# The mixer's output projection of an encoder layer by seven block products, with the operands' forms in the buffers of the normed input

## The chip, the cores and the metric

The kernel runs on one core of one Trainium2 chip. The metric is the time of one execution in microseconds of the device, from the start of the program to its end. A change of about 0.2% can be told from none. All inputs and weights lie in HBM as float32; the weights are packed on the host into blocks of 128 partitions x 1024 columns.

## The reference, cut to what matters

One encoder layer on 512 tokens of width 1024, with 256 memory tokens:

```python
# per layer
x = x + token_mixer(rmsnorm(x, norm_mix), ...)       # 4 HGRN2 heads and 4 mLSTM heads, each 128 wide
x = x + cross_attention(rmsnorm(x, norm_xattn), rmsnorm(mem, norm_mem), w_q, w_kv, w_o)
x = x + squared_relu_mlp(rmsnorm(x, norm_mlp), w_up, w_down)
return rmsnorm(x, norm_final)

# the last line of token_mixer: the projection that the change is about
return jnp.concatenate([hgrn_out, mlstm_out], axis=-1) @ w_out     # (512 x 1024) @ (1024 x 1024)
```

`cross_attention` takes its keys and values from the memory tokens by `w_kv`, its queries from `rmsnorm(x)` by `w_q`, and projects its heads by `w_o`. The mixer's heads are scans over chunks in the reference; the kernel computes them in blocks of 128 tokens.

## The kernel before

**Precision.** Every large matmul is done as three: both operands are split into a high part (a rounding copy on ScalarE) and a low part (the difference, on VectorE), and high x high, high x low and low x high are added in one PSUM bank. `split_out` (line 258) is the split, `mm3` (lines 260 to 263) the three matmuls. Rows of both engines at L258 are therefore splits, of weights (`wh`, `wl`) or of activations.

**Weights.** `SEQ` is the order in which weight blocks come. `load(i)` has SP fetch block i into one of three `st` buffers (L236); `split(i)` makes its `wh` and `wl`, three buffers each; `weights` asks for a block and two more ahead.

**Chains.** The heads are generators (`hgrn_pair`, `mlstm_chain`) in the list `chains`; the projections call `tick()` every few matmuls, which moves one of two chains on by a step. So the heads' small operations stand among the matmuls of a projection, and a scheduler then sets the order on each engine. `drain()` runs what is left.

**Stages around the change.** 0 to 240 us: input projection and HGRN heads. 240 to 318 us: the mLSTM heads' queries and keys (`qk_proj`, with a convolution in `conv_evac`, L746), then the memory's keys (`kv`, eight products of 128x256 whose PSUM banks `mm` are split into the buffers `a4`) and values (four of 128x512), with the first two mLSTM heads beside them. An mLSTM head is: decay rows (L774, L777, L779, buffer `as`), four value products (L789, buffers `sm`), a denominator by tiny operations on VectorE and the GpSimd power (L795 to L802, L197, L199), and `head_out`: scale (L595), four transposes (L602), gate (L603), and the split of the result into `ys[idx]`, a `yT` buffer. `ys[0..3]` are the HGRN heads, `ys[4..7]` the mLSTM heads, each with 128 features on the partitions and 512 tokens in columns, high and low part beside each other.

318 to 349 us: the memory's values and the third and fourth mLSTM head. From 349 us: the output projection, `proj_res("out", ...)` at line 949. It goes over two halves of the output's columns, and in each over four row tiles of 128 tokens, with 8 k tiles of 128 features: the first half takes k tiles 0 to 3 (the HGRN heads) for all row tiles first, then `heads_done` drains the chains, then k tiles 4 to 7. Each finished 128x512 bank is added to the residual `xr[t, c]` (L924, buffers `vv`), its squares are summed on ScalarE, and four transposes turn it into `x2T` (L938, buffers `xT`), which the query projection `xq` of the cross-attention reads.

**Buffers.** PSUM has four `mm` and four `sm` banks. In SBUF there are two `xT` pairs-of-halves (first the normed input `xs`, last read by `qk_proj(1)`, then `x2T`), ten `a4` of 128x1024, two `gate` of 128x1024 (the gates of two HGRN or mLSTM heads each; the last two mLSTM heads read theirs until their L603), two `as`.

**By blocks.** The cross-attention's output projection (`xo`) and the second matrix of the MLP (`down`) are already done by `by_blocks`: a product of 2x2 blocks (tokens in two halves, features in two halves, columns in two halves) from seven products of blocks instead of eight. Some of the seven have a block as an operand, others a sum of blocks; sums of weight blocks are made by POOL DMAs that add into a buffer (`add_block`, L1065), sums of the heads by VectorE where the heads are made. Each product adds its result into one or two of the four output blocks (`INTO`).

Of the kernel before, what the change touches and what calls it, by code (L numbers as in the profile page):

```python
# [18 lines left out]
P = 128  # L19
# [26 lines left out]
def _split_order():  # L46
# [15 lines left out]
    seq += t("out", 0, 0) + t("out", 0, 512)  # L62
# [8 lines left out]
    seq += t("xo", 0, 512, 2)  # L71
# [5 lines left out]
NSTREAM = len(SEQ) - 10  # L77
# [3 lines left out]
def trunk(ctx: ExitStack, tc: tile.TileContext, x, mem, wpk, vec, cst, lmask, rmask, rows, out):  # L81
# [505 lines left out]
    def head_out(o, gate, gcol, idx):  # L587
# [17 lines left out]
        split_out(ys[idx][0], ys[idx][1], gate)  # L605
        yield

# [146 lines left out]
    def mlstm_chain(h, gate):  # L754
# [28 lines left out]
        for wt in range(4):  # L783
# [19 lines left out]
            if wt % 2 == 1:  # L803
                yield
        yield from head_out(ho, gate, V_MN + h, 4 + h)


    hst = {}
    pace = [2]
    scored = set()  # L810
# [76 lines left out]
    list(qk_proj(1))  # L887
    mlstm_start(1, mo1)
# [13 lines left out]

    xr = {}
# [6 lines left out]
    def heads_done():  # L910
        drain()
        load_xr(1)

    load_xr(0)
# [4 lines left out]

    def proj_res(mat, k0, src, tgt, st, pre=None, late=False):  # L920

        for c in range(2):
            for t, ps in proj_t(mat, k0, 512 * c, src, pre=pre if c == 0 else None, late=late and c == 0):
                v.tensor_tensor(out=xr[t, c], in0=ps, in1=xr[t, c], op=ALU.add)  # L924
                stats(st, t, c)
                transp(tgt, t, c)

    def transp(tgt, t, c):
        dst, gcol = tgt
        ps = smb()  # L930
        for k in range(4):
            pe.transpose(ps[:, k * P:k * P + P], xr[t, c][:, k * P:k * P + P], ident)
        for k in range(4):
            g = vc[:, gcol + 4 * c + k:gcol + 4 * c + k + 1]
            hi = dst[c][:, k * 1024 + t * P:k * 1024 + t * P + P]
            lo = dst[c][:, k * 1024 + 512 + t * P:k * 1024 + 512 + t * P + P]
            sc.activation(hi, ps[:, k * P:k * P + P], AF.Copy, scale=g)
            v.scalar_tensor_tensor(out=lo, in0=ps[:, k * P:k * P + P], scalar=g, in1=hi.bitcast(F32), op0=ALU.mult, op1=ALU.subtract)  # L938
# [9 lines left out]
    x2T = XT()  # L948
    proj_res("out", 0, ys, (x2T, V_XATTN), st1, heads_done, True)
# [86 lines left out]

    ORDER = ("P1", "P2", "P6", "P5", "P7", "P3", "P4")
    LATE = [(p, g) for p in ORDER[2:] for g in range(2)]  # L1040
    JOBS = {f: [("P1", 0), ("P2", 0), ("P1", 1), ("P2", 1)] + LATE for f in range(4)}

    JOBS[-1] = [(p, g) for p in ("P1", "P7", "P2", "P5", "P6", "P3", "P4") for g in range(2)]
    jobs_hl, sums, q_made = {}, {}, [None]

    def block(f, g, kh, c):
        return SIDX["t", "down" if f >= 0 else "xo", max(f, 0) * 8 + 2 * g + 4 * kh, 512 * c]

    def sum_loads(f, names):

        parts = {"T2": ((0, 1), (1, 1), (0, 0)), "U": ((0, 1), (0, 0)), "T3": ((0, 1), (1, 1))}
        for nme in names:
            if nme == "T3":
                t2 = [G4()[:, :] for _ in range(2)]
            else:
                t = A16()
                t2 = [t[:, g * 1024:g * 1024 + 1024] for g in range(2)]
            for g in range(2):
                sums[f, nme, g] = t2[g]
        return [add_block(sums[f, nme, g], block(f, g, *parts[nme][i]), i > 0)  # L1060
                for i in range(3) for nme in names for g in range(2) if i < len(parts[nme])]

    def add_block(dst, idx, accumulate=True):
        kw = dict(accum_op=ALU.add) if accumulate else {}
        return gp.dma_start(out=dst, in_=wpk[idx], **kw)  # L1065
# [5 lines left out]
    def job(f, n):  # L1071

        if n >= len(JOBS[f]):
            if f < 3:
                split(SIDX["d", "up", 0, 1024 * (f + 1)] + n - len(JOBS[f]))
# [350 lines left out]
```

## Time and profile before

| what | value |
|---|---|
| time, median of 3 runs | 847.56 us (847.48 to 848.4) |
| the profiled execution's own time | 847.43 us |
| its span in the trace | 845.3 us |
| granted TensorE clock, mean | 0.998 |
| HBM read, written | 116.00 MB, 2.10 MB |
| VectorE weight splits (L258, 128x1024 from `st`) | 131, mean 1224 ns |
| ScalarE's part of them | 131, mean 1060 ns |

How to read it: the span runs from the first to the last instruction; the 2 us between it and the execution's time lie around it. A busy share is the share of the span in which an engine had an instruction running. TensorE's matmuls are pipelined, so that a matmul shows a longer busy time than the step to the next one. In a timeline each row has the start, the busy time, engine, source line, operation, output and inputs, and in brackets the idle time ahead of the instruction with what ended it. In a table of windows each row has the length, and then for PE, PEld (weight loads), DVE (VectorE), ACT (ScalarE) and POOL the busy time with its number of instructions, the granted clock, the DMA share and GB/s.

### The profile page before, as it was taken

The page shows a single profiled execution, that of the slowest core. Times are in us where ns is not written, and L with a number is a line of the kernel's source. Part 1 is how long each engine was busy: PE and PEld are TensorE (multiplying, and loading weights), DVE is VectorE, ACT ScalarE, POOL GpSimd, SP SyncE. Part 2 cuts the span into 40 slices and gives each one's busy share as a digit, 9 for nine tenths or more (in the row PEclk, how much of TensorE's full clock was granted, in tenths as well). Part 3 has the DMA queues.
Part 4 walks back from the last instruction along what each step waited for, and adds up shares of the span by engine and source line. Part 5 has one row for each costly group of instructions (what it writes and reads, how often), then busy time and mean ns, then how long its engine had stood idle before and what let it go on. Part 6 is the DMA issues. An engine that isn't in the chain of part 4 may idle for free.

```text
span 845.3 us, 11740 instructions
## 1 busy us (share of the span) xinstructions
PE 834.2 (99%) x4434; PEld 689.3 (82%) x4434; DVE 589.3 (70%) x1025; ACT 433.6 (51%) x779; POOL 77.5 (9%) x130
## 2 busy tenths in 40 slices
PE   8999999999999999999999999999999999999996
PEld 6787888887977987888888888888888888888885
DVE  6568875599457987655557896776677656866685
ACT  5246454443578576454455575543454444434544
POOL 2000000100010000100010004103101210221001
PEclk9999999999999999999999999999999999999999
DMA  7342124122152332452261447968935993698332
GB/s 275 111 131 86 65 77 133 43 88 86 64 149 75 101 125 100 152 147 77 89 160 50 100 100 263 261 173 238 279 107 136 278 257 100 166 278 210 114 79 100
DMA packets 34122, 118.86 MB, mean 141 GB/s; under 512 B 3921, under 2 KB 4049, under 8 KB 34066
## 3 DMA queue, kind: packets, MB, share of 16 engines
q1 hardware_dynamic: 22832, 77.80, 26.8%
q0 software_dynamic: 10944, 39.85, 21.2%
q8 instruction: 35, 0.57, 0.3%
q10 hardware_dynamic: 290, 0.47, 0.2%
q14 instruction: 21, 0.17, 0.1%
HBM read 116.00 MB, written 2.10 MB: 140 GB/s over the span
## 4 chain that ended last, share of the span: by engine, by line
PE 90%; issue 5%; DVE 2%; DMA 1%; ACT 1%; POOL 1%; POOLq 0%; ACTq 0%; DVEq 0%
PE mm L261 18%; PE mm L262 18%; PE mm L263 18%; PE sm L1118 6%; PE sm L1116 6%; PE sm L1117 6%; PE sm L485 2%; PE sm L789 2%; PE mm L1118 2%; PE mm L1116 2%; PE mm L1117 2%; PE sm L774 2%; PE sm L555 2%; PE sm L263 1%; PE sm L262 1%
## 5 line engine op out<-in xcount | busy, mean ns | idle before, releaser
L258 ACT ACTIVATE wh<-st 128x1024 fp32r<-128x1024 f32 x131 | 138.6, 1060 | 190.2 <-PE mm L262 119.0
L258 DVE TENSOR_TENSOR wl<-st,wh 128x1024 fp32r<-128x1024 f32 x131 | 160.1, 1224 | 86.7 <-ACT wh L258 85.8
L261 PE MATMUL mm<-xT,wh 128*128 128x512 f32 x544 | 216.1, 398 | 0.0
L262 PE MATMUL mm<-xT,wh 128*128 128x512 f32 x544 | 212.8, 391 | 0.3 <-DVE xT L938 0.3
L263 PE MATMUL mm<-xT,wl 128*128 128x512 f32 x544 | 212.7, 391 | 0.1
L262 PEld LDWEIGHTS mm<-xT,wh 128*128 128x128 f32 x544 | 102.2, 188 | 22.1 <-issue 1.0
L263 PEld LDWEIGHTS mm<-xT,wl 128*128 128x128 f32 x544 | 102.1, 188 | 21.9 <-DVE wl L258 0.3
L261 PEld LDWEIGHTS mm<-xT,wh 128*128 128x128 f32 x544 | 102.2, 188 | 21.8 <-issue 0.7
L1065 POOL DMA_DIRECT2D as<-in_wpk x52 | 39.7, 765 | 250.8 <-DVE wl L258 165.8
L1305 DVE SCALAR_TENSOR_TENSOR t<-mm,rg 128x512 f32<-128x512 f32 x32 | 22.0, 691 | 52.2 <-PE mm L263 52.0
L1116 PE MATMUL sm<-wh,yT 128*128 128x512 f32 x128 | 49.8, 389 | 0.0
L1117 PE MATMUL sm<-wl,yT 128*128 128x512 f32 x128 | 49.8, 389 | 0.0
L1118 PE MATMUL sm<-wh,yT 128*128 128x512 f32 x128 | 49.8, 389 | 0.0
L258 ACT ACTIVATE wh<-as 128x1024 fp32r<-128x1024 f32 x26 | 27.6, 1062 | 37.0 <-PE sm L1118 23.7
L258 DVE TENSOR_TENSOR wl<-as,wh 128x1024 fp32r<-128x1024 f32 x26 | 31.9, 1226 | 14.0 <-ACT wh L258 14.0
L199 POOL TENSOR_TENSOR tiny<-tiny,misc 128x4 f32<-128x4 f32 (+1 forms) x10 | 9.6, 964 | 269.0 <-DVE tiny L197 269.0
L1116 PE MATMUL sm<-wh,a 128*128 128x512 f32 x84 | 32.9, 391 | 0.0
L1118 PE MATMUL sm<-wh,a 128*128 128x512 f32 x84 | 32.7, 389 | 0.0
L1117 PE MATMUL sm<-wl,a 128*128 128x512 f32 x84 | 32.7, 389 | 0.0
L1248 DVE TENSOR_TENSOR vv<-vv,sm 128x512 f32<-128x512 f32 x48 | 31.0, 680 | 1.7 <-PE sm L1118 1.7
L1117 PEld LDWEIGHTS sm<-wl,yT 128*128 128x128 f32 x128 | 24.0, 188 | 5.0
L1118 PEld LDWEIGHTS sm<-wh,yT 128*128 128x128 f32 x128 | 24.0, 188 | 5.0
(316 smaller groups left out, 1590.3 us busy)
## 6 DMA issues: line engine op xcount, KB each, us to landing
st<-in_wpk SPq DMA_DIRECT2D x131, 512.0 KB, 3.4
as<-in_wpk POOLq DMA_DIRECT2D x52, 512.0 KB, 7.0
gate<-in_wpk POOLq DMA_DIRECT2D x24, 512.0 KB, 7.2
as<-in_x SPq DMA_DIRECT2D x4, 512.0 KB, 6.7
vv<-in_x SPq DMA_DIRECT2D x8, 256.0 KB, 3.4
out<-vv SPq DMA_DIRECT2D x7, 256.0 KB, 2.2
a<-in_mem SPq DMA_DIRECT2D x2, 512.0 KB, 4.2
t<-in_rows SPq DMA_DIRECT2D x2, 256.0 KB, 4.9
```

The costliest lines, as they stand in the source:

```text
L258: return sc.activation(dst_hi, src, AF.Copy), v.tensor_tensor(out=dst_lo, in0=src, in1=dst_hi.bitcast(F32), op=ALU.subtract)
L261: pe.matmul(ps, lhsT=ah, rhs=bh, start=first, stop=False)
L262: pe.matmul(ps, lhsT=ah, rhs=bl, start=False, stop=False)
L263: pe.matmul(ps, lhsT=al, rhs=bh, start=False, stop=last)
L485: mm = pe.matmul(ps[64 * i:64 * i + 64, z:z + 64], lhsT=kc[j][:, w * P + 64 * i:w * P + 64 * i + 64], rhs=rhs(j, w * P, i), start=True, st ...
L555: pe.matmul(ps[:, t * P:t * P + P], lhsT=A[j][:, s * 512 + t * P:s * 512 + t * P + P], rhs=vh[s][:, h * P:h * P + P], start=(s == 0), stop ...
L1065: return gp.dma_start(out=dst, in_=wpk[idx], **kw)
L1116: pe.matmul(ps, lhsT=ah, rhs=bh, start=new, stop=False, **fl)
L1117: pe.matmul(ps, lhsT=ah, rhs=bl, start=False, stop=False, **fl)
L1118: pe.matmul(ps, lhsT=al, rhs=bh, start=False, stop=end and k == 1, **fl)
L1248: added = v.tensor_tensor(out=z, in0=z, in1=ps, op=ALU.add if sign > 0 else ALU.subtract)
L1305: v.scalar_tensor_tensor(out=y, in0=ps, scalar=0.0, in1=rrow[:, 0:512], op0=ALU.max, op1=ALU.mult)
```

## The change

The output projection of the mixer is done by `by_blocks`, as `xo` and `down` are, under the number -2: seven products in the order P1, P7, P2, P5, P6, P3, P4, each as two jobs of 12 matmuls (`g`: two k tiles each), on heads p and 4 + p as the two halves of the features. Its parts:

- `mix_start` makes from each HGRN head the difference of its token halves (first the sum of high and low part, L619, then the difference, L620, then a split into the buffer `xT`). It is called after `qk_proj(1)`, when the normed input is no longer read, and the two `xT` buffers taken then become `x2T` later.
- `mix_forms`, at the end of `head_out` of each mLSTM head, makes the three other forms (five operations of 256 columns, L633 to L637, and two splits), also into `xT`.
- The weight sums are T3 and U, in two halves (g) each. Of T3 the first half, and of U the first half in part, are added by POOL DMAs. The second half of each is made by `quick_sum`: two loads by SP and an addition on VectorE (L1175). That of U is loaded into a `gate` buffer.
- Each product adds its bank into the residual (L1113), 18 additions in all where there were 8; the transposes are made for two row tiles at a time; the first two column blocks of `xq` are taken together with the halves of the features in reversed order (`first_two`, which was the MLP's own).
- The order of the `out` weight blocks in `SEQ` is another, and two of them are no longer in the stream.

```diff
+        if idx >= 4:
+            formers.append((idx - 4, gate))
+            mix_forms()
...
+    def mix_start():
+        for p in range(4):
+            h, l = [t.bitcast(F32) for t in ys[p]]
+            e = T2()[:, 0:512]
+            v.tensor_tensor(out=e, in0=h, in1=l, op=ALU.add)
+            v.tensor_tensor(out=e[:, 0:256], in0=e[:, 0:256], in1=e[:, 256:512], op=ALU.subtract)
+            s3 = mixT[0][:, p * 512:p * 512 + 256], mixT[0][:, p * 512 + 256:p * 512 + 512]
+            split_out(*s3, e[:, 0:256])
+            sta_m[p].update(P1=tuple(t[:, 0:256] for t in ys[p]), P7=s3)
...
+    def mix_forms():
+        while mixT and formers:
+            p, m = formers.pop(0)
...
+            v.tensor_tensor(out=sa1, in0=x2h, in1=m2, op=ALU.subtract)
+            v.tensor_tensor(out=sa1, in0=sa1, in1=x2l, op=ALU.add)
+            v.scalar_tensor_tensor(out=sa2, in0=eh, scalar=-1.0, in1=m2, op0=ALU.mult, op1=ALU.subtract)
+            v.tensor_tensor(out=sa2, in0=sa2, in1=el, op=ALU.subtract)
+            v.tensor_tensor(out=s4, in0=m1, in1=sa2, op=ALU.add)
+            ya = mixT[1][:, p * 1024:p * 1024 + 1024]
+            split_out(ya[:, 0:512], ya[:, 512:1024], sa)
...
+            split_out(yh, yl, s4)
...
     list(qk_proj(1))
+    x2T = XT()
+    mixT += x2T
+    mix_start()
+    mix_forms()
     mlstm_start(1, mo1)
...
+    JOBS[-2] = JOBS[-1] = [(p, g) for p in ("P1", "P7", "P2", "P5", "P6", "P3", "P4") for g in range(2)]
...
+    sums[-2, "T3", 0] = G4()[:, :]
+    add_block(sums[-2, "T3", 0], block(-2, 0, 0, 1), False)
+    add_block(sums[-2, "T3", 0], block(-2, 0, 1, 1))
...
-    proj_res("out", 0, ys, (x2T, V_XATTN), st1, heads_done, True)
...
+    def quick_sum(nme, g, t, b0, b1):
+        other = A16()[:, 0:1024]
+        for dst, b in ((t, b0), (other, b1)):
+            nc.sync.dma_start(out=dst, in_=wpk[block(-2, g, *b)])
+        v.tensor_tensor(out=t, in0=t, in1=other, op=ALU.add)
+        sums[-2, nme, g] = t[:, :]
+
+    def mix_ready(p, g):
+        if (p, g) == ("P1", 0):
+            while len(valued) < 4:
+                tick1()
+            quick_sum("T3", 1, A4(), (0, 1), (1, 1))
+            sums[-2, "U", 0] = A4()[:, :]
+            nc.sync.dma_start(out=sums[-2, "U", 0], in_=wpk[block(-2, 0, 0, 1)])
+        if (p, g) == ("P7", 1):
+            load_xr(1)
+        if (p, g) == ("P2", 0):
+            drain()
+            add_block(sums[-2, "U", 0], block(-2, 0, 0, 0))
+            quick_sum("U", 1, G4(), (0, 1), (0, 0))
+            while waiting:
+                waiting.pop(0)()
+            fixed.enter_context(tc.manual_schedule(engines={mybir.EngineType.PE}))
...
+    by_blocks(-2, sta_m, (mm2, mm2, sm2, sm2), add_1, mix_ready, mix_after)
```

How the change moves instructions is seen on three engines. First VectorE while the memory's keys are projected. `as_331` is a decay buffer of the first mLSTM head (its line L779 before is L820 after), `a4` the buffers of the keys, `mm` their PSUM banks, `t2` the scratch of the forms, `xT_365` the buffer that the forms go to. Before:

```order
L779 TENSOR_TENSOR as_331_2273<-as_331_2273,sm_364_2474 128x512
L795 TENSOR_SCALAR tiny_375_2508<-sm_374_2502 128x2
L751 SCALAR_TENSOR_TENSOR yT_342_2344<-t2_362_2462,t2_361_2458 128x512
L796 TENSOR_TENSOR tiny_375_2508<-tiny_375_2508,sm_374_2502 128x2
L258 TENSOR_TENSOR a4_365_2478<-mm_372_2488,a4_365_2478 128x256
L258 TENSOR_TENSOR wl_416_2718<-st_405_2666,wh_415_2717 128x1024
```

After, from the same operation to the same bank's split (here `mm_378`):

```order
L820 TENSOR_TENSOR as_331_2273<-as_331_2273,sm_364_2474 128x512
L619 TENSOR_TENSOR t2_367_2480<-yT_204_1413 128x512
L792 SCALAR_TENSOR_TENSOR yT_342_2344<-t2_362_2462,t2_361_2458 128x512
L258 TENSOR_TENSOR wl_422_2740<-st_411_2688,wh_421_2739 128x1024
L620 TENSOR_TENSOR t2_367_2480<-t2_367_2480 128x256
L619 TENSOR_TENSOR t2_368_2485<-yT_214_1486 128x512
L258 TENSOR_TENSOR xT_365_2478<-t2_367_2480,xT_365_2478 128x256
L620 TENSOR_TENSOR t2_368_2485<-t2_368_2485 128x256
L619 TENSOR_TENSOR t2_369_2490<-yT_288_2085 128x512
L258 TENSOR_TENSOR xT_365_2478<-t2_368_2485,xT_365_2478 128x256
L620 TENSOR_TENSOR t2_369_2490<-t2_369_2490 128x256
L619 TENSOR_TENSOR t2_370_2495<-yT_290_2107 128x512
```

All sums (L619) and three differences (L620) of the HGRN heads' forms stand here, with two of their splits into `xT_365`. On the same engine it goes on without a gap:

```order
L258 TENSOR_TENSOR wl_434_2813<-st_423_2743,wh_433_2812 128x1024
L258 TENSOR_TENSOR xT_365_2478<-t2_369_2490,xT_365_2478 128x256
L620 TENSOR_TENSOR t2_370_2495<-t2_370_2495 128x256
L836 TENSOR_SCALAR tiny_381_2530<-sm_380_2524 128x2
L258 TENSOR_TENSOR a4_371_2500<-mm_378_2510,a4_371_2500 128x256
```

Where three rows stood between the decay's product and the split of the bank, there are now fifteen: the forms of the four HGRN heads with three of their splits, the convolution's product, two weight splits and a tiny operation.

TensorE in the same stage: `mm_424` is the fourth product of the keys, `mm_436` the fifth, which takes the bank that the split above empties; `sm_391` before and `sm_397` after are the first value products of the first mLSTM head. Before, where the fourth product (there `mm_418`) ends:

```order
L261 MATMUL mm_418_2723<-a4_312_2173,wh_387_2573 128x256
L789 MATMUL sm_391_2592<-vv_249_1813,as_325_2233 128x129
L789 MATMUL sm_391_2592<-vv_250_1822,as_325_2233 128x129
L789 MATMUL sm_391_2592<-vv_252_1857,as_325_2233 128x129 x2
L789 MATMUL sm_391_2592<-vv_253_1866,as_325_2233 128x129
L262 MATMUL mm_418_2723<-a4_312_2173,wh_387_2573 128x256
```

After (six more matmuls of `mm_436`, on `a4_309`, stand directly ahead of the first row, and the last of `mm_424` ahead of them):

```order
L261 MATMUL mm_436_2818<-a4_310_2171,wh_409_2684 128x256
L262 MATMUL mm_436_2818<-a4_310_2171,wh_409_2684 128x256
L263 MATMUL mm_436_2818<-a4_310_2171,wl_410_2685 128x256
L261 MATMUL mm_436_2818<-a4_310_2171,wh_409_2684 128x256
L830 MATMUL sm_397_2614<-vv_249_1813,as_325_2233 128x129
L830 MATMUL sm_397_2614<-vv_250_1822,as_325_2233 128x129
L830 MATMUL sm_397_2614<-vv_252_1857,as_325_2233 128x129 x2
L830 MATMUL sm_397_2614<-vv_253_1866,as_325_2233 128x129
```

The value products now stand behind the first ten matmuls of the fifth key product, where they stood inside the fourth.

The third place is VectorE in the output projection, where U's second half is made: `gate_569` is the buffer that the weights are loaded to, `gate_282` the same memory as the gates of the last two mLSTM heads, `vv` the residual, `mm` and `sm` the products' banks. Before, in the second half of the columns:

```order
L924 TENSOR_TENSOR vv_524_3288<-mm_530_3297,vv_524_3288 128x512
L938 SCALAR_TENSOR_TENSOR xT_527_3294<-sm_554_3413,vc_68,xT_527_3294 128x128 x2
L938 SCALAR_TENSOR_TENSOR xT_527_3294<-sm_556_3441,vc_68,xT_527_3294 128x128 x2
L924 TENSOR_TENSOR vv_525_3290<-mm_531_3298,vv_525_3290 128x512
L938 SCALAR_TENSOR_TENSOR xT_527_3294<-sm_556_3441,vc_68,xT_527_3294 128x128 x2
```

After, from the last form on:

```order
L637 TENSOR_TENSOR t2_556_3417<-gate_282_2059,t2_555_3416 128x256
L258 TENSOR_TENSOR xT_366_2479<-t2_555_3416,xT_366_2479 128x512
L258 TENSOR_TENSOR xT_365_2478<-t2_556_3417,xT_365_2478 128x256
L1113 TENSOR_TENSOR vv_564_3452<-vv_564_3452,sm_557_3428 128x512
L1113 TENSOR_TENSOR vv_535_3334<-vv_535_3334,sm_557_3428 128x512
L1113 TENSOR_TENSOR vv_565_3454<-vv_565_3454,sm_558_3429 128x512
L1113 TENSOR_TENSOR vv_536_3336<-vv_536_3336,sm_558_3429 128x512
L1175 TENSOR_TENSOR gate_569_3479<-gate_569_3479,as_570_3480 128x1024
L1113 TENSOR_TENSOR vv_533_3330<-vv_533_3330,mm_571_3488 128x512
L1113 TENSOR_TENSOR vv_534_3332<-vv_534_3332,mm_572_3489 128x512
L258 TENSOR_TENSOR wl_576_3507<-gate_569_3479,wh_575_3506 128x1024
```

The last reader of the old gates, the sum into the same memory and the split of the sum stand in this order, with additions into the residual between them.

More of the change, by code (lines that the diff above doesn't have):

```diff
@@ L900, in trunk, with block @@
             mvx[t, c] = d
+    ORDER = ("P1", "P2", "P6", "P5", "P7", "P3", "P4")
+    LATE = [(p, g) for p in ORDER[2:] for g in range(2)]
+    JOBS = {f: [("P1", 0), ("P2", 0), ("P1", 1), ("P2", 1)] + LATE for f in range(4)}
+    JOBS[-2] = JOBS[-1] = [(p, g) for p in ("P1", "P7", "P2", "P5", "P6", "P3", "P4") for g in range(2)]
+    jobs_hl, sums, q_made, waiting = {}, {}, [None], []
+    def block(f, g, kh, c):
+        return SIDX["t", "down" if f >= 0 else "xo" if f == -1 else "out", max(f, 0) * 8 + 2 * g + 4 * kh, 512 * c]
@@ L1049, in sum_loads @@
[L1049 to L1061, printed above, removed]
```

354 lines of the change are left out of this document (188 added, 166 removed).

## The prediction

> **What bounds the kernel now.** I read the summary first, then the chain that ended last, then windows around the output projection, then the timelines of TensorE and VectorE there.
>
> ```profile
> span 845.3 us, 11740 instructions
> PE 834.2 (99%) x4434; PEld 689.3 (82%) x4434; DVE 589.3 (70%) x1025; ACT 433.6 (51%) x779; POOL 77.5 (9%) x130
> PE 90%; issue 5%; DVE 2%; DMA 1%; ACT 1%; POOL 1%; POOLq 0%; ACTq 0%; DVEq 0%
> 280.00:290.00 10.00, 10.00 (x88) 9.97 (x87) 9.87 (x20) 3.30 (x5) 0.00 (x0) 1.00 0.33 106
> 290.00:300.00 10.00, 9.94 (x86) 9.76 (x85) 8.59 (x43) 5.51 (x21) 0.43 (x1) 1.00 0.31 107
> 300.00:310.00 10.00, 9.56 (x76) 9.07 (x75) 8.56 (x15) 6.47 (x14) 1.62 (x2) 1.00 0.31 107
> 310.00:318.00 8.00, 8.00 (x39) 6.21 (x38) 5.20 (x6) 7.87 (x22) 0.00 (x0) 1.00 0.40 132
> 318.00:349.00 31.00, 31.00 (x165) 24.72 (x165) 21.52 (x67) 18.47 (x55) 1.25 (x2) 1.00 0.36 124
> ```
>
> TensorE has no idle time to give: 99% busy, 90% of the chain. So a matmul taken away is worth its step, and a wait put in front of TensorE costs its length. The windows (length, then busy PE, PEld, DVE, ACT, POOL, the granted clock) show who could cause one. From 280 to 310 us, where the memory's keys are projected while the first two mLSTM heads finish, VectorE is busy 9.87, 8.59 and 8.56 of 10 us; from 318 to 349 it has a third to spare.
>
> **What goes.** Before, the projection is 192 matmuls of 128x512 (4 row tiles, 2 column halves, 8 k, 3 products of halves); now 14 jobs of 12, so 168.
>
> ```profile
> 349.23 0.39 PE L261 MATMUL mm<-wh,yT 128*128 128x512 f32 x1
> 351.72 0.39 PE L263 MATMUL mm<-wh,yT 128*128 128x512 f32 x1
> 351.95 0.60 PE L602 MATMUL sm<-cs,t 128*128 128x128 f32 x4
> 352.31 0.48 PE L261 MATMUL mm<-wh,yT 128*128 128x512 f32 x1
> 353.55 0.40 PE L263 MATMUL mm<-wh,yT 128*128 128x512 f32 x1
> 354.01 0.50 PE L261 MATMUL mm<-wh,yT 128*128 128x512 f32 x1
> ```
>
> The twelve matmuls of the first two row tiles start between 349.23 and 351.72, the next instruction at 351.95: 2.72/12 = 0.227 us a step, though each shows 0.39 busy. Twenty-four fewer: **-5.4 us**. A job of 12 is 2.72, a head's four transposes 0.36. The 32 transposes of the result stay. Between 353.55 and 354.01 a step takes 0.46; the wait of 0.2 in it goes with the old order of the weights.
>
> **What comes on VectorE ahead of the projection.** The forms of the four HGRN heads (four sums and four differences, four splits) now stand among the kv stage's work, and each mLSTM head brings five differences and two splits more. Steps of VectorE, start to next start:
>
> ```profile
> 286.75 0.75 DVE L746 SCALAR_TENSOR_TENSOR t<-t,vc,t 128x512 f32<-128x512 f32 x1
> 287.41 0.68 DVE L779 TENSOR_TENSOR as<-as,sm 128x512 f32<-128x512 f32 x1
> 288.01 0.15 DVE L795 TENSOR_SCALAR tiny<-sm 128x2 f32<-128x2 f32 x1
> 288.88 0.15 DVE L796 TENSOR_TENSOR tiny<-tiny,sm 128x2 f32<-128x2 f32 x1
> 288.95 0.42 DVE L258 TENSOR_TENSOR a<-mm,a 128x256 fp32r<-128x256 f32 x1
> 325.71 0.41 DVE L777 TENSOR_TENSOR as<-as,sm 128x256 f32<-128x256 f32 x1
> 326.04 0.55 DVE L779 TENSOR_TENSOR as<-as,sm 128x384 f32<-128x384 f32 x1
> 352.14 1.22 DVE L258 TENSOR_TENSOR wl<-st,wh 128x1024 fp32r<-128x1024 f32 x1
> 353.27 0.68 DVE L258 TENSOR_TENSOR a<-mm,a 128x512 fp32r<-128x512 f32 x1
> 353.87 0.74 DVE L603 SCALAR_TENSOR_TENSOR gate<-sm,vc,gate 128x512 f32<-128x512 f32 x1
> ```
>
> So 0.60 for 512 columns, 0.66 for 512 with a scalar, 0.33 for 256, 1.14 for 1024, 0.07 for a tiny one that waits for nothing (288.88 to 288.95). The four HGRN heads cost 4 x (0.60 + 0.33 + 0.33) = 5.0 us, an mLSTM head 5 x 0.33 + 0.60 + 0.33 = 2.6. Two of these fall before 318 us: 10.2 us more on VectorE. Sums of this shape from two operands in SBUF have no row here; 128x1024 goes by the split's 1.14 (from one operand's pass at worst twice that, 2.3), the others by the rows above.
>
> ```profile
> 292.06 0.28 PE L261 MATMUL mm<-a,wh 128*128 128x256 f32 x1
> 292.18 1.28 PE L789 MATMUL sm<-vv,as 128*128 128x129 f32 x10
> 296.54 2.47 PE L789 MATMUL sm<-vv,as 128*128 128x129 f32 x20
> 298.77 0.36 PE L263 MATMUL mm<-a,wl 128*128 128x256 f32 x1
> 300.64 0.69 DVE L595 TENSOR_TENSOR t<-t,tiny 128x512 f32<-128x512 f32 x1 [0.69 <-POOL tiny L199]
> 301.48 0.63 PE L602 MATMUL sm<-cs,t 128*128 128x128 f32 x4 [0.44 <-ACT t L801]
> 311.23 0.40 PE L261 MATMUL mm<-wh,a 128*128 128x512 f32 x1
> ```
>
> The order of VectorE is the same as before up to the L779 at 287.41. Behind it stood the tiny operations and, at 288.95, the split that empties the PSUM bank of the first kv block. Now that split has ahead of it four 512 sums, the conv's product (0.66), two weight splits, four differences, three splits of 256 and a tiny: 2.40 + 0.66 + 2.28 + 1.32 + 0.99 + 0.07 = 7.7 us, so it starts at 295.7 and ends at 296.1. The fifth kv block takes this bank, one of four. TensorE reaches it three matmuls of 0.12 us after 292.06 (the value matmuls of 292.18 now stand later), at 292.4, and **waits 3.7 us**. Then 10 matmuls (1.2) bring it to 297.3; the next value matmuls want the bank that the first ones' L843 frees, 2.4 us of rows after 295.7: 298.1. Four of them (2.23 for two) and 16 matmuls later it is 304.5, and there stand the transposes of the first mLSTM head. Its L843 starts some 4.5 us after 298.0 by 5 steps of 0.27 and about twenty tiny ones between 0.07 and 0.19, at 302.5; from there to the transposes it took
>
> ```profile
> 347.62 0.35 DVE L802 SCALAR_TENSOR_TENSOR t<-sm,tiny,t 128x128 f32<-128x128 f32 x1 [0.49 <-ACT t L801]
> 348.44 0.17 DVE L197 TENSOR_SCALAR tiny<-tiny 128x4 f32<-128x4 f32 x1 [0.47 <-ACT t L593]
> 349.79 0.69 DVE L595 TENSOR_TENSOR t<-t,tiny 128x512 f32<-128x512 f32 x1 [1.19 <-POOL tiny L199]
> 350.40 1.22 DVE L258 TENSOR_TENSOR wl<-st,wh 128x1024 fp32r<-128x1024 f32 x1
> ```
>
> 0.82 + 1.35, and 0.84 more (300.64 to 301.48): 305.5. Before they ran at 301.48 with five kv matmuls (0.6) more behind them: 4.6 us late. The forms of the two heads follow; the split that frees the bank of the first 128x512 product stands 11.2 us behind 306.0 (three weight splits, four operations of 512 and two of them with a scalar among it), at 317.2 to 318, where that product began at 311.23: 6.0 to 6.8 late. I take **+6.4 us**. It cannot be less than 10.2 minus VectorE's idle time from 290 to 318 (1.41 + 1.44 + 2.80), 4.5; waits for ScalarE, which I left out of most steps, could make it 8. TensorE is full from there to 349, so nothing is won back; VectorE catches up there.
>
> **What comes in the projection.** Call its first matmul T. The second half of the weight sum U, which P5 wants (the seventh and eighth job in the order of jobs), is put into the gate buffer of the last two mLSTM heads, loaded by SP, added on VectorE, and only then split.
>
> ```profile
> st<-in_wpk SPq DMA_DIRECT2D x131, 512.0 KB, 3.4
> as<-in_wpk POOLq DMA_DIRECT2D x52, 512.0 KB, 7.0
> L258 ACT ACTIVATE wh<-as 128x1024 fp32r<-128x1024 f32 x26 | 27.6, 1062 | 37.0 <-PE sm L1118 23.7
> ```
>
> The last head's scaling L595 ended at T+1.2 (350.40); now it stands behind another weight split on ScalarE, so T+1.2 to T+2.2. From there to the last read of the gate VectorE has 25 rows: 5 weight splits and one sum (6.84), 6 of 512 columns (3.72 with the scalar), 14 of 256 (4.7), 15.3 us, with 0.6 of waits for ScalarE T+17.5. The load lands 3.4 later, T+20.9; the sum takes 1.14, ScalarE 1.06, the split on VectorE 1.14, with 0.1 at two hand-overs: T+24.4. TensorE reaches the second matmul of that job after seven jobs, two transposes and one matmul: 19.0 + 0.7 + 0.3 = T+20.3 with a small wait ahead of the second P7 job (its weight sum, too, is made on VectorE: **+0.3**). So a wait of **4.1 us** (3.2 to 4.9 with the two ends of L595 and one wait more or less). The blocks for U's first half and T3 go through POOL at 7.0 us each: they land near T+11.4, and are wanted at T+17, so they are hidden by some 5 us; if that cover went, the same wait would only come earlier. The 18 additions into the rows (10 more than the 8 before, 6 us) and six more splits stand in this stage on VectorE, and the same scheme stands in the later xo projection:
>
> ```profile
> 480.00:490.00 10.00, 10.00 (x46) 8.15 (x45) 9.64 (x18) 6.24 (x11) 0.86 (x1) 1.00 0.01 2
> ```
>
> VectorE at 9.64 there and TensorE still full, so I charge them nothing beyond the queue of the 25 rows. SP stands behind the gate's load as well; what it blocks are weights of the next stage, wanted 25 us later.
>
> **Sum**, on the profiled execution (847.43 us, span 845.3; the median of the runs is 847.56): -5.4 - 0.2 + 6.4 + 0.3 + 4.1 = +5.2, so 852.6; by the median **852.7**. Its own range is 849.3 (4.5 and 3.2, the rest equal, a little less for the old 0.3 wait at the end of the stage) to 855.5 (8 and 4.9).
>
> **Rivals.**
> *TensorE keeps its pace* (the other side): the queue of forms on VectorE is absorbed, because the banks are freed in time. For it: at 94% and more VectorE let TensorE run in xo. Against: the order puts 7.7 us of rows ahead of one bank's release, and TensorE needs it 4.4 us after 288.01. It decides at that bank: with under 4.4 us ahead of the split there is no wait. If no wait arises in either place: -5.6, 842.0. Chance 9%.
> *One of the two waits is hidden*: -5.6 + 6.7 = 848.7 with the kv one alone, 846.1 with the fifth product's alone. For it: each rests on one buffer. 12%.
> *The clock falls in the waits.* TensorE's granted clock is 1.00 in every window above, and after its start no wait of it there exceeds 0.44 us, so no row shows what a wait of 4 us does to it. If the job after each wait ran at half pace, two jobs of 2.72 would take 5.4 us more: 858. 6%. [...]
> *The change does not do what it says*: the order has 168 matmuls in the stage and two sums on VectorE, so nothing is kept for this.
>
> **Numbers.** The forecast has 73%, the three rivals 9, 12 and 6. Less than 0.2% (1.7 us, about what a measurement of this kernel can tell from no change) is 845.9 to 849.3: faster 9%, same 13%, slower 78%. A range of 846.0 to 856.5 leaves out the first rival, the clock, and about 5% of the forecast's own tail.
>
> **What would show it.** In the changed profile: TensorE waiting for VectorE's `a` split near 292 to 296 us; L602 of the first mLSTM head at 305 to 306; the projection's first matmul at 355 to 356; a wait of some 4 us ahead of the second half of P5, released by the weight split behind the sum of line 1175; 5.4 us less of 128x512 matmuls. I am wrong if TensorE stays full from 288 to 318, or if the gate's sum is there before P5 wants it.

## The result: slower by 1.5%

The changed kernel takes 861.07 us (median of 4, 859.44 to 861.83), the kernel before 847.8 beside it; the ratio is 1.0153, with a 95% interval of 1.0135 to 1.0171. The prediction had the direction, slower, and both places; the time lies outside its range of 846.0 to 856.5. The profiled execution took 860.77 us with a span of 859.0, 13.7 more than before.

**The page.** The span, the busy times and the chain that ended last:

```profile
span 859.0 us, 11778 instructions
PE 834.5 (97%) x4410; PEld 689.6 (80%) x4410; DVE 617.2 (72%) x1067; ACT 440.4 (51%) x781; POOL 83.0 (10%) x137
PE 88%; DVE 5%; DMA 2%; ACT 2%; issue 1%; POOL 1%; POOLq 0%; SPq 0%; ACTq 0%; DVEq 0%
```

TensorE has 24 matmuls less and yet the same busy time, 834.5 us against 834.2, so there must be matmuls that take longer. And its idle time rose from 11.1 us (845.3 less 834.2) to 24.5. VectorE has 28 us more. The windows of the two stages show where (columns as before: length, PE, PEld, DVE, ACT, POOL, granted clock, DMA share, GB/s):

```profile
290.00:300.00 10.00, 6.14 (x42) 5.92 (x41) 9.60 (x29) 3.74 (x10) 0.00 (x0) 0.85 0.34 112
300.00:310.00 10.00, 8.97 (x76) 8.80 (x76) 7.36 (x33) 6.56 (x26) 1.04 (x1) 0.98 0.01 2
310.00:320.00 10.00, 8.09 (x63) 7.55 (x63) 9.09 (x20) 5.06 (x8) 1.39 (x1) 1.00 0.34 111
...
360.00:370.00 10.00, 7.86 (x38) 5.93 (x36) 8.00 (x12) 2.84 (x4) 2.54 (x3) 1.00 0.82 222
370.00:380.00 10.00, 9.63 (x41) 7.60 (x42) 9.14 (x17) 4.32 (x7) 0.84 (x1) 1.00 0.87 211
380.00:390.00 10.00, 5.74 (x17) 4.06 (x16) 9.21 (x12) 4.18 (x7) 2.26 (x3) 0.79 0.33 107
390.00:400.00 10.00, 10.00 (x40) 8.12 (x39) 5.95 (x7) 4.41 (x7) 0.85 (x1) 0.87 1.01 228
```

Before, each of these had PE at 9.56 or more and a clock of 1.00. Now there are two holes, at 290 to 320 and at 360 to 390, and behind the deeper part of each the granted clock is below 1.

**The keys of the memory.** VectorE's rows around the split that frees a bank (the row of `a<-mm,a`), then TensorE's around the bank's next user:

```profile
288.15 0.68 DVE L820 TENSOR_TENSOR as<-as,sm 128x512 f32<-128x512 f32 x1
288.75 0.68 DVE L619 TENSOR_TENSOR t<-yT 128x512 f32<-128x512 f32 x1
...
296.62 0.41 DVE L258 TENSOR_TENSOR a<-mm,a 128x256 fp32r<-128x256 f32 x1
```

```profile
293.04 0.28 PE L263 MATMUL mm<-a,wl 128*128 128x256 f32 x1
297.18 0.55 PE L261 MATMUL mm<-a,wh 128*128 128x256 f32 x1 [3.86 <-ACT xT L258]
297.53 0.41 PE L262 MATMUL mm<-a,wh 128*128 128x256 f32 x1
...
299.45 5.17 PE L830 MATMUL sm<-vv,as 128*128 128x129 f32 x40
...
307.56 0.63 PE L602 MATMUL sm<-cs,t 128*128 128x128 f32 x4 [1.03 <-DVE t L595]
```

The split ends at 297.03 and the fifth key product starts 0.15 us behind it, after 3.86 us of idleness. The releaser that the profile names, a split on ScalarE into `xT`, is a neighbour of the true one: the bank is freed by the split on VectorE, and the first experiment below moves what stands ahead of it. The matmuls behind the wait take 0.21 us a step, not 0.12, at a granted clock of 0.50 from 297.5 to 300.

**The projection.** Its first matmul starts at 358.07 (349.23 before). TensorE ahead of the second jobs of P7 and P5, then the two sums on VectorE and the loads they need:

```profile
366.97 0.39 PE L1036 MATMUL sm<-wh,xT 128*128 128x512 f32 x1
368.90 0.50 PE L1034 MATMUL sm<-wh,xT 128*128 128x512 f32 x1 [1.54 <-ACT wh L258]
370.16 0.50 PE L1035 MATMUL sm<-wl,xT 128*128 128x512 f32 x1 [0.76 <-DVE wl L258]
...
381.29 0.39 PE L1036 MATMUL sm<-wh,xT 128*128 128x512 f32 x1
385.19 0.51 PE L1034 MATMUL sm<-wh,xT 128*128 128x512 f32 x1 [3.51 <-ACT wh L258]
386.45 0.80 PE L1035 MATMUL sm<-wl,xT 128*128 128x512 f32 x1 [0.76 <-DVE wl L258]
387.04 0.63 PE L1036 MATMUL sm<-wh,xT 128*128 128x512 f32 x1
```

```profile
358.98 0.33 SPq L236 DMA_DIRECT2D st<-in_wpk  x1
359.41 0.38 SPq L1174 DMA_DIRECT2D a<-in_wpk  x1
...
366.45 1.23 DVE L1175 TENSOR_TENSOR a<-a,as 128x1024 f32<-128x1024 f32 x1 [1.15 <-DMA a<-in_wpk]
...
379.34 0.33 SPq L1174 DMA_DIRECT2D gate<-in_wpk  x1
...
380.13 2.48 DVE L1113 TENSOR_TENSOR vv<-vv,sm 128x512 f32<-128x512 f32 x4
382.74 1.23 DVE L1175 TENSOR_TENSOR gate<-gate,as 128x1024 f32<-128x1024 f32 x1
```

T3's load is issued at 359.41, directly behind a weight load that SP's queue held until 358.98, and lands some 7 us later. U's is issued at 379.34 behind the last read of the gates. Mark the last two rows: VectorE was busy with four additions until 382.6, and the load landed at about the same time. So two things kept that sum, and the profile can show only one of them.

### The profile page after: what moved, and what is told of

Its sections match the earlier page's. It is cut to its first block, busy times and chain, and to the rows that moved or that the text cites. A ratio compares the mean times of both kernels' runs of the same rounds, so it can differ in the third digit from the quotient of the medians.

```text
span 859.0 us, 11778 instructions
## 1 busy us (share of the span) xinstructions
PE 834.5 (97%) x4410; PEld 689.6 (80%) x4410; DVE 617.2 (72%) x1067; ACT 440.4 (51%) x781; POOL 83.0 (10%) x137
## 4 chain that ended last, share of the span: by engine, by line
PE 88%; DVE 5%; DMA 2%; ACT 2%; issue 1%; POOL 1%; POOLq 0%; SPq 0%; ACTq 0%; DVEq 0%
PE mm L261 17%; PE mm L263 17%; PE mm L262 17%; PE sm L1035 6%; PE sm L1036 6%; PE sm L1034 6%; PE sm L485 2%; PE mm L1036 2%; PE mm L1035 2%; PE mm L1034 2%; PE sm L815 2%; PE sm L555 2%; DVE wl L258 2%; DMA a<-in_wpk 1%; PE sm L1125 1%
## 5 line engine op out<-in xcount | busy, mean ns | idle before, releaser
L258 ACT ACTIVATE wh<-st 128x1024 fp32r<-128x1024 f32 x129 | 136.4, 1059 | 183.7 <-PE mm L262 121.7
L258 DVE TENSOR_TENSOR wl<-st,wh 128x1024 fp32r<-128x1024 f32 x129 | 157.7, 1224 | 75.4 <-ACT wh L258 74.9
L262 PEld LDWEIGHTS mm<-xT,wh 128*128 128x128 f32 x544 | 102.3, 188 | 21.2 <-issue 1.0
L977 POOL DMA_DIRECT2D gate<-in_wpk x28 | 21.1, 755 | 123.4 <-DVE wl L258 92.4
L258 ACT ACTIVATE wh<-gate 128x1024 fp32r<-128x1024 f32 x18 | 19.0, 1060 | 23.0 <-PE sm L1036 13.2
```

What stands on the lines that cost most here:

```text
L258: return sc.activation(dst_hi, src, AF.Copy), v.tensor_tensor(out=dst_lo, in0=src, in1=dst_hi.bitcast(F32), op=ALU.subtract)
L262: pe.matmul(ps, lhsT=ah, rhs=bl, start=False, stop=False)
```

## The experiments

Each was timed against the kernel before on the same chip. The theory drawn from the profiles: (1) the forms ahead of the bank's split, (2) the gate buffer ahead of U's sum, (3) idle waits halve the clock.

### The forms behind the keys

```diff
     list(qk_proj(1))
-    x2T = XT()
-    mixT += x2T
-    mix_start()
-    mix_forms()
     mlstm_start(1, mo1)
...
+    x2T = XT()
+    mixT += x2T
+    mix_start()
+    mix_forms()
     mvx = {}
     for c in range(2):
         for t, ps in proj_t("kv", 0, 1024 + 512 * c, ms, 2):
```

> Only the place of mix_start is changed: the forms of the HGRN heads are asked for between the memory's keys and its values, not ahead of the keys. Theory (forms ahead of the split that empties a PSUM bank): the wait of 3.86 us at 293 us and the half clock behind it go, the projection's first matmul stands at 349 to 351 us (358.07 in the changed kernel, 349.23 before), and the time falls by 7 to 8.8 us, to 852 to 854. Rival 1 (10 us more on VectorE cost TensorE their length wherever they stand): the first matmul stays at 357 to 359, the time at 860 to 862. Rival 2 (the stage's loss comes from the half clock alone, the wait itself being there in another form): the first matmul at 353 to 355, 856 to 858.

851.9 us, 1.0049 (1.0034 to 1.0064) of before. The kv stage is as before, with no wait over 0.43 us, and the projection:

```profile
345.25 0.39 PE L1034 MATMUL mm<-wh,yT 128*128 128x512 f32 x1
...
376.28 0.79 PE L1034 MATMUL sm<-wh,xT 128*128 128x512 f32 x1 [3.37 <-ACT wh L258]
377.54 0.79 PE L1035 MATMUL sm<-wl,xT 128*128 128x512 f32 x1 [0.47 <-DVE wl L258]
378.13 0.63 PE L1036 MATMUL sm<-wh,xT 128*128 128x512 f32 x1
```

9.2 us are gone with one block of code moved down by one loop, and the same forms cost TensorE no wait between 311 and 345 us. Rival 1 is out: it was the place in VectorE's order. The 9.2 us are a balance: 8.8 ahead of the projection and 2.7 at P7's second job are gone, and two waits inside P1 for the heads' scaling, 0.79 and 1.66 us, are new. (The first matmul of the projection now stands among value products of the last heads, hence 345.25.) The waits of P5 and the half clock are still there.

### The buffer of U's sum alone

```diff
+        if t is None:
+            pair = A16()
+            t, other = pair[:, 0:1024], pair[:, 1024:2048]
...
-            quick_sum("U", 1, G4(), (0, 1), (0, 0))
+            quick_sum("U", 1, None, (0, 1), (0, 0))
```

> Only the buffer of U's second half is changed: both its operands lie in one decay buffer (as) and not in the gate buffer that the last head still reads. Theory (the load waits for the last read of the gates): the wait ahead of the second job of P5 (3.67 and 1.03 us over the step) goes, and with it the half clock of 385.2 to 392.3 us, which costs 3.2: 861.1 - 7.9 = 853.2, 852 to 855. Rival 1 (the sum is late because VectorE is behind, whatever the buffer): the wait stays over 3 us, 859 to 862. Rival 2 (the clock falls in this stage without a wait too): 856 to 857.

861.31 us, as the changed kernel. The theory falls in its simple form. The time is that of Rival 1, but the wait isn't over 3 us, as that one had it. The timeline has the load of U's second half, ScalarE's split of the first half, the sum, and TensorE at P5's second job:

```profile
361.93 0.42 SPq L1178 DMA_DIRECT2D as<-in_wpk  x1
...
376.97 1.06 ACT L258 ACTIVATE wh<-a 128x1024 fp32r<-128x1024 f32 x1 [3.83 <-DMA a<-in_wpk]
...
385.41 1.21 DVE L1179 TENSOR_TENSOR as<-as 128x1024 f32<-128x1024 f32 x1
...
387.85 0.50 PE L1034 MATMUL sm<-wh,xT 128*128 128x512 f32 x1 [1.68 <-ACT wh L258]
```

The load now issues 17 us earlier (361.93), yet the sum runs at 385.41: it stands on VectorE behind the last head's forms and four additions. The wait shrank from 3.51 to 1.68 us only. What was won was given back: the DMA share is higher (1.01 and 0.99 in the two 8 us from 364, 0.81 and 0.86 in the changed kernel), ScalarE waits 3.83 us for U's first half, and P2 waits 1.13 and 0.61 us for the last head's split behind it on VectorE, with the clock at half from 380.0 to 383.4 us. That the earlier load is what delays U's first half fits these rows; no run takes it alone.

### TensorE kept busy in the wait

```diff
+            if (f, p, g, u) == (-2, "P5", 1, 0):
+                for _ in range(15):
+                    pe.matmul(held[user[p]][u], lhsT=zero, rhs=ys[4][0], start=False, stop=False, ...)
```

> Fifteen matmuls of 128x512 with a weight of zeros stand ahead of the second job of P5 (they add zero to its bank; 3.4 us of work in a wait of 3.7), all else as in the changed kernel. Theory (the clock is halved because TensorE idled): the job starts as late as before, within 0.5 us, but at full clock, and the time falls by 3.2 us to 857.5 to 858.5, with the granted clock 1.00 from 384 to 394 us. Rival 1 (the clock falls for another reason than idleness, such as the load of the stage): 861 to 862, clock 0.50 as before. Rival 2 (the fillers are not in the wait): up to 864.5.

857.05 us, 4.0 less than the changed kernel. TensorE's rows, with line numbers shifted by 2 to 5, and the window behind the wait, here and then in the changed kernel:

```profile
381.49 3.66 PE L1032 MATMUL sm<-yT,zero 128*128 128x512 f32 x15
385.21 0.50 PE L1039 MATMUL sm<-wh,xT 128*128 128x512 f32 x1
386.47 0.50 PE L1040 MATMUL sm<-wl,xT 128*128 128x512 f32 x1 [0.76 <-DVE wl L260]
386.81 0.39 PE L1041 MATMUL sm<-wh,xT 128*128 128x512 f32 x1
```

```profile
386.00:388.00 2.00, 1.53 (x7) 1.27 (x8) 2.00 (x3) 2.00 (x5) 0.72 (x2) 1.00 0.02 6
```

```profile
386.00:388.00 2.00, 1.55 (x4) 1.26 (x5) 2.00 (x3) 2.00 (x5) 0.73 (x2) 0.50 0.06 8
```

P5's second job starts at 385.21 where it had started at 385.19, and at a clock of 1.00 where it was 0.50. Fifteen useless matmuls make the kernel faster: the loss behind the wait is the clock, and idleness is its cause. The spans of the two profiled executions, 859.0 and 856.2 us, differ by 2.8, near the 3.0 that the half clock costs by its steps (last table); the rest of the 4.0 lies within what the executions of the changed kernel differ by.

### All three moves

Forms behind the keys, and T3's and U's second halves each with both operands in a decay buffer.

```diff
-            quick_sum("T3", 1, A4(), (0, 1), (1, 1))
+            quick_sum("T3", 1, None, (0, 1), (1, 1))
...
-            quick_sum("U", 1, G4(), (0, 1), (0, 0))
+            quick_sum("U", 1, None, (0, 1), (0, 0))
```

> The forms behind the keys, and both sums made on VectorE (T3's and U's second halves) with their two operands in one decay buffer each. Theory (the three waits and the two half clocks are all that the change loses): 861.1 - 8.8 - 7.9 - 2.6 = 841.8, 841 to 844, faster than the kernel before by 0.4 to 0.8 %. Rival 1 (VectorE's work of 28 us more finds no room between 311 and 385 us): new waits there, 846 to 850. Rival 2 (one of the two other theories falls): as that run shows, 850 or more.

854.74 us, 1.0085 (1.007 to 1.01), slower than the first move alone. The time is that of Rival 2: P5 still waits 3.15 us with U's buffer free. A new wait, as Rival 1 has it, comes on top, and the rows show how: T3's sum, asked for ahead of the last head's scaling, sits on VectorE and waits for its load, and the head stands behind it (VectorE, then TensorE):

```profile
357.22 1.23 DVE L1179 TENSOR_TENSOR as<-as 128x1024 f32<-128x1024 f32 x1 [1.75 <-DMA as<-in_wpk]
...
360.87 0.88 PE L602 MATMUL sm<-cs,t 128*128 128x128 f32 x4 [3.50 <-DVE t L595]
...
379.88 0.50 PE L1034 MATMUL sm<-wh,xT 128*128 128x512 f32 x1 [3.15 <-ACT wh L258]
```

So a new theory: both the buffer and the place in VectorE's order hold U's sum, and the next experiment moves both.

### U's sum ahead of the last head's forms

```diff
         if (p, g) == ("P1", 0):
...
+            two = A16()
+            two_blocks("U", 1, two[:, 0:1024], two[:, 1024:2048], (0, 1), (0, 0))
+        if (p, g) == ("P1", 1):
+            add_two("U")
...
+            first = v.tensor_tensor(out=sa1, in0=x2h, in1=m2, op=ALU.subtract)
+            if p == 3:
+                for b in made_two.values():
+                    behind(first, b)
```

`two_blocks` issues the loads of `quick_sum`, `add_two` its addition; `behind` sets the last head's first form after both sums on VectorE.

> As e_late, and U's second half has both operands in one decay buffer, loaded with T3's, and its sum stands on VectorE ahead of the last head's forms (in e_late it stands behind these and behind six additions). Theory (the wait ahead of P5's second job was two waits one behind the other: the buffer, and the place of the sum in VectorE's order; e_u took the first alone): the wait of 3.54 and 0.8 us goes with the half clock behind it (11 steps of 0.43 in place of 0.23, 2.2 us): 851.9 - 6.5 = 845.4, 844.5 to 847. Rival 1 (the sum ahead of the forms pushes these back, and P2 or P5 waits for a head's form): 848 to 852. Rival 2 (neither place nor buffer, the split's own order counts): 851 to 853.

847.4 us, 0.9999 (0.9989 to 1.0009): 4.5 less than the first move alone, 2.0 short of the forecast and just outside its range. P5's wait and the half clock are gone, and a piece of Rival 1 is there, P2 waiting for the last head:

```profile
369.62 0.50 PE L1037 MATMUL mm<-wh,yT 128*128 128x512 f32 x1 [1.32 <-ACT yT L258]
```

### The last heads' transposes later

```diff
-        if parts[0] % 2 == 0:
+        if parts[0] % 2 == 0 and parts[0] >= 4:
             tick()
```

> As e_sum_early, and the transposes of the third mLSTM head stand behind all of P1, those of the fourth behind the first job of P7, not inside P1 where they wait 0.79 and 1.66 us for the heads' scaling in e_late. Theory (those waits cost their length): 2.4 us less than e_sum_early, 842.5 to 844, which is faster than the kernel before by 0.4 to 0.6 %. Rival (the heads' forms come 2 to 3 us later and P2's second job or P5 waits for them): 845 to 848.

849.51 us, 1.0022 (1.0012 to 1.0031), slower than without: the rival's wait, at a time 1.5 us above its range. The two waits inside P1 went, and came back at P2:

```profile
367.34 0.50 PE L1039 MATMUL mm<-wh,yT 128*128 128x512 f32 x1 [1.27 <-DVE yT L258]
369.33 0.73 PE L1037 MATMUL mm<-wh,yT 128*128 128x512 f32 x1 [1.49 <-ACT yT L258]
```

The second of these is followed by a granted clock of 0.50 from 370 to 372 us, though neither wait reached 1.5. The rival had counted no half clock.

### How long a wait halves the clock

Six of the zero matmuls in place of fifteen, on the kernel with the forms behind the keys.

```diff
-                for _ in range(15):
+                for _ in range(6):
```

> As e_late, with six of the matmuls that add zero ahead of P5's second job (1.4 us of work in a wait of 3.5). Theory A (the clock is halved only by an idle stretch of over 3 us): the stretch left is 2.1 us, the clock stays at 1.00 from 374 to 384 us, the time falls by 2 to 2.5 us to 849.4 to 850. Theory B (idle time adds up with the next short wait, as in e_u, where a wait of 1.7 us with another of 0.8 was followed by a half clock): the clock falls all the same, 851 to 852.

851.08 us, and neither theory alone: the nine executions run from 848.96 us (mean granted clock 0.998) to 852.22 (0.993). The profiled one is of the second kind:

```profile
376.80 0.70 PE L1039 MATMUL sm<-wh,xT 128*128 128x512 f32 x1 [2.06 <-ACT wh L260]
378.06 0.79 PE L1040 MATMUL sm<-wl,xT 128*128 128x512 f32 x1 [0.56 <-DVE wl L260]
378.65 0.63 PE L1041 MATMUL sm<-wh,xT 128*128 128x512 f32 x1
```

The clock is at half for 6.8 us behind this wait (0.73, 0.50, 0.50 and 0.56 in the four 2 us from 376). The executions at 848.96 and 849.33 us, with a mean clock of 0.998, weren't profiled; they fit the same wait with a clock that doesn't fall, so that the fall costs some 3 us. That is inferred from the times and the mean clocks alone.

### U's second half off VectorE

```diff
         if (p, g) == ("P1", 0):
...
+            sums[-2, "U", 1] = A16()[:, 0:1024]
+            nc.sync.dma_start(out=sums[-2, "U", 1], in_=wpk[block(-2, 1, 0, 1)])
...
+        if (p, g) == ('P7', 0):
+            behind(add_block(sums[-2, "U", 1], block(-2, 1, 0, 0)), powed[-1][1])
...
-            quick_sum("U", 1, G4(), (0, 1), (0, 0))
```

> As e_late, and U's second half is not added on VectorE: one operand is loaded by SP into a decay buffer, the other added by a POOL DMA behind the last head's power; U's first half is added earlier, and T3's sum stands behind the last head's mean (L197), not ahead of it. Theory (what is left of the loss in the projection is VectorE's queue: 1.14 us of sum less, and the head's scaling 0.6 us earlier): no wait ahead of P5, P2's wait for the last head's split (1.32 us in e_sum_early) falls to under 0.5: 847.4 - 0.6 - 1.2 = 845.6, 844.5 to 846.5, faster than before. Rival (the POOL DMA issues at about 358 us and takes 7 us or more beside the others, so U's half lands at 366 or later): a wait of 1 to 3 us ahead of P5's second job, 847 to 850.

846.24 us, 0.9984 (0.9975 to 0.9992): faster than both kernels, by a margin near what can be told, and within the forecast. TensorE waits inside P1, 0.23 us in P2 and 0.43 us at 382. Three things moved at once here (U's second half, its first half, the place of T3's sum); their shares can't be told apart. What VectorE has in the stage, with the forms moved and one sum less:

```profile
360.00:370.00 10.00, 9.77 (x44) 7.73 (x43) 9.82 (x17) 4.54 (x6) 1.79 (x2) 1.00 0.94 229
370.00:380.00 10.00, 10.00 (x46) 8.23 (x45) 9.86 (x16) 4.94 (x6) 2.25 (x3) 1.00 0.55 123
```

In the same windows of the kernel before, VectorE was busy 4.18 and 6.35 us.

### Two tries at the rest

With the last heads' transposes behind P1 and half of P7's first job:

```diff
-        if parts[0] % 2 == 0:
+        if parts[0] > 3:
             tick()
```

> As e_u_pool, and the transposes of the last two heads stand behind P1 and behind the first half of the first job of P7. Theory: the two waits of 0.8 and 1.7 us for the heads' scaling go, 2 us less than e_u_pool: 843 to 844.5. Rival (as e_turns_late showed, the last head's split then comes later than P2's second job): the wait comes back there, with a half clock if it reaches 2 to 3 us: 847 to 850.

847.08 us, 0.9989 (0.9979 to 0.9998): the rival again, P2's second job waits 1.76 us. With the transposes behind P1 and all of P7's first job, and the third head's forms behind the fourth's gate:

```diff
-            mix_forms()
+            if idx != 6:
+                mix_forms()
...
-        if parts[0] % 2 == 0:
+        if parts[0] % 2 == 0 and parts[0] >= 4:
             tick()
```

> As e_u_pool, and the transposes of the last two heads stand behind P1 and behind the first job of P7, and the forms of the third head behind the gate of the fourth, so that VectorE makes the last head's split ahead of them. Theory (what TensorE still waits for in e_u_pool, 0.8, 1.7 and 0.2 us, is the last head's chain, and VectorE's order decides how long it is): the last split comes at 365 us, ahead of P2's second job, and 2.4 us go: 843.5 to 844.5. Rival (the forms, 2 to 3 us later, are then late for P5): a wait there of 1 to 3 us, 845.5 to 848.

848.24 us, 1.0009 (1.0 to 1.0018): now P5 waits for a form.

```profile
375.76 0.50 PE L1037 MATMUL sm<-wh,xT 128*128 128x512 f32 x1 [2.98 <-ACT xT L260]
```

```profile
360.00:370.00 10.00, 9.33 (x41) 7.72 (x42) 10.00 (x15) 4.86 (x7) 1.79 (x2) 1.00 0.96 235
370.00:380.00 10.00, 6.69 (x23) 4.53 (x22) 9.94 (x19) 4.48 (x9) 2.25 (x3) 0.88 0.77 166
```

Three orders, and the wait went from the transposes to P2 and to P5: what is late is whatever stands last on VectorE. The last run takes work away from it; it leaves out forms that the result needs, and so tells only what they cost:

```diff
             p, m = formers.pop(0)
+            if p >= 2:
+                yh, yl = ys[4 + p]
+                sta_m[p].update(sta_m[p - 2], P1=sta_m[p]["P1"], P7=sta_m[p]["P7"])
+                sta_m[p].update(P2=(yh[:, 0:256], yl[:, 0:256]), P4=(yh[:, 256:512], yl[:, 256:512]))
+                continue
```

> As e_head_first, without the forms of the third and fourth mLSTM head (five operations and two splits each, 5.2 us of VectorE); P5, P6 and P3 take the forms of the first two heads in their place, so that the output is not the reference's. All matmuls, loads and sums are there. Theory (VectorE, at 4.9 to 5.0 of every 5 us from 360 to 380, is the bound of what is left): the wait of 2.98 us ahead of P5's second job goes with its half clock, 843.5 to 845. Rival (the sum by the POOL DMA, or the weights' order, holds P5): the wait stays, 847 to 848.5.

844.59 us, 0.9968 (0.9956 to 0.998): the wait is gone, 3.65 us with it. VectorE was busy 10.00 and 9.94 us of the two 10 us from 360 with the forms, and is 10.00 and 7.66 without: there it was the limit.

## Why the prediction was wrong

The direction, the two places and the queue on VectorE that causes each came out. The sum failed in two of its terms above all: the half clock, which it put at nothing (4.4 us), and the wait at P7's second job, which it put at 0.3 us (2.7).

| term, us | forecast | measured in the changed kernel |
|---|---|---|
| 24 matmuls less | -5.4 | -5.4 (steps of 0.227 where the clock is 1.00) |
| start of the projection | +6.4 | +8.8 (358.07 - 349.23) |
| second job of P7 | +0.3 | +2.7 (steps 1.93 and 1.26, less two of 0.227) |
| wait of the old order | -0.2 | -0.2 (P1's first twelve steps are 0.227 each) |
| second job of P5 | +4.1 | +4.7 (3.90 and 1.26, less two of 0.227) |
| half clock behind P5's wait | 0 | +3.0 (13 steps of 0.427 from 387.04 to 392.59 and one of 0.59, where 0.227 is full) |
| sum | +5.2 | +13.6 (the span: +13.7) |

**Fewer matmuls: right**, by the trace's steps.

**Kv stage: right mechanism, term too small.** The bank's split was put at 295.7 to 296.1 and came at 296.62 to 297.03; the wait of 3.7 was 3.86 idle. Moving the forms alone took every wait over 0.43 us out of this stage, so the cause is shown. What was missing in +6.4 are the half clock behind the wait (ten steps of 0.21 for 0.12, and forty value matmuls in 4.93 us for 4.46: 1.4 us) and what is left, some 1.0 us, at the heads' transposes (the first at 307.56, forecast at 305.5) and at the bank of the first 512-wide product (320.02, forecast at 317.2 to 318).

**P7's second job: the term was mis-sized, 0.3 for 2.7.** It counted the sum on VectorE and nothing for its load, which SP's queue issued at 359.41 and which took some 7 us; VectorE sat 1.15 us for it. The two steps of the split behind the sum then stand in TensorE's path. With the forms moved, the load is issued at 341.74 and the wait is gone.

**P5's second job: right size, 4.7 for 4.1, and only half the cause.** The prediction named the gate buffer. Its walk of VectorE's 25 rows gave the read of the gates and then the load; that the sum's own place in the order was as late, it did not say. That the size fits is in part luck: from the projection's first matmul on, the last read of the gates ended after 21.2 us (forecast 17.5), and TensorE reached the job's second matmul after 23.4 (forecast 20.3), both late. Taking away the buffer alone brought nothing in total; with the forms moved, buffer and place together brought 4.5 us.

**The clock: a rival at 6%, and it decided the size.** Its price of 5.4 us was near the 4.4 measured (1.4 and 3.0). Half pace was the author's assumption, and it came near what was measured: steps of 0.427 us where 0.227 is full, at a granted clock of 0.50. The prediction gave the case almost no weight, though both of its own waits, 3.7 and 4.1 us, were longer than any that the trace before shows behind the start (0.44 us at the longest). Here the clock is 1.00 or 0.50 (a window across a change shows a value between, such as 0.76 from 296 to 298 us), it fell behind both waits (3.86 and 3.51 us), and the filled wait kept it at 1.00. With both the clock (4.4) and the P7 term right, the forecast would have been 859.5.

**The range.** The ends of the forecast's own range, 849.3 and 855.5, don't come out of its terms: 4.5 and 3.2 give 849.9, or 849.6 without the old wait of 0.3, and 8 and 4.9 give 855.1. Nothing hangs on the difference.

**The other rivals.** "TensorE keeps its pace" is out, and so is "one of the two waits is hidden": both waits were there, and a third at P7.

## What to carry to other kernels

An algorithm that trades matmuls for vector work moves the bound when VectorE has no room in that very stage: 5.4 us of TensorE were bought here with 28 us of VectorE, and the best order found kept 1.3 of them. Where work is put in an engine's order can matter more than how much it is: moving the first forms was worth 9.2 us here, leaving out those of two heads 3.65. Look for the bank release, or the head's scaling, that stands behind it. And count a wait of TensorE at more than its length: the waits of 3.86 and 3.51 us here had 1.4 and 3.0 us of half clock behind them, as in the table, and fifteen matmuls put in the second kept the clock at 1.00.

## What the runs showed of the hardware that was not expected

- Fifteen matmuls with a zero operand, 3.66 us of TensorE's time in a wait, made the kernel 4.0 us faster.
- The clock fell after waits of very different length: after 3.86 and 3.51 us in the changed kernel, but also after 2.06 us (the dose), after 1.27 and 1.49 us with a single matmul between (the last heads' transposes later), and after 1.13 and 0.61 us with two between (the buffer of U's sum alone). Waits of nearly one size went either way: the clock stayed at 1.00 after 1.54 and 0.76 us at P7's second job in the changed kernel, and fell after 1.68 and 0.76 us at P5's with U's buffer alone (0.56 from 390 to 392 us). What decides between the two, no run shows.
- The stretches at half clock lasted 3.4 or 6.8 us. From 285 to 445 us (from 340 us with the third head's forms behind the fourth's gate, and without the forms) the thirteen profiles have thirteen of them: eight of 3.4 us and five of 6.8. The changed kernel has one of each, 297.0 to 300.4 and 385.8 to 392.6 us. The same wait of 3.86 us ahead of the fifth key product was followed by 3.4 us in the changed kernel and by 6.8 us in two kernels that are like it up to there (the buffer of U's sum alone, and TensorE kept busy), where the projection starts at 359.70 and 359.27 in place of 358.07. So the 1.4 us charged to this half clock belong to the profiled execution, and a part of the spread below may come from there.
- The changed kernel's four executions spread over 2.4 us, those of the best version (eleven) over 0.5: with no wait above 1.7 us in its profile, its clock was 0.997 or 0.998 in each.
- A DMA of 512 KB landed 3.3 us after its issue where no other was issued within 5 us (`gate<-in_wpk` from SP, 379.34), and some 7 us after where two other loads of SP and one by POOL were issued within 4 us (`a<-in_wpk`, 359.41).
